# A two-layer diffusion trunk on one core: TensorE in program order, modulation in pairs of steps, a gate summed one stage earlier, and merged boundary evictions

## The chip, the core and the metric

The kernel runs on one core of a Trainium2 chip. The metric is the device time of one execution in microseconds (us), and the time of a kernel is the median of its runs. The core has five instruction streams that matter here: TensorE (PE, matrix products, with its weight loads shown apart as PEld), VectorE (DVE), ScalarE (ACT), GpSimd (POOL) and SyncE (SP, which only issues transfers). Each works through its own list of instructions in order and waits on semaphores for the others. On-chip data lies in SBUF; PE writes its results to PSUM, of which the kernel uses eight banks of 128 partitions x 512 fp32.

## The reference

The input is 512 "sample" tokens and 128 "prompt" tokens of width 1024. Two layers follow; each has a channel mixer, a token mixer (a gated recurrence, RG-LRU, in layer 0; windowed averages in layer 1) and a second channel mixer. Every mixer reads a normalised and modulated input and adds a gated, normalised output to the residual x:

```python
def _layer(x, mod, l, norm_g, ffn_w1, ffn_w3, ffn_w2, mixer):
    sh1, sc1, g1, sh2, sc2, g2, sh3, sc3, g3 = jnp.split(mod[:, None, :], N_MOD, axis=-1)
    h = _modulate(_rmsnorm(x, norm_g[l, 0]), sh1, sc1)                 # x * (1 + scale) + shift
    x = x + 0.5 * g1 * _rmsnorm(_swiglu(h, ffn_w1[l, 0], ffn_w3[l, 0], ffn_w2[l, 0]), norm_g[l, 1])
    h = _modulate(_rmsnorm(x, norm_g[l, 2]), sh2, sc2)
    y, st = mixer(h)                                                   # RG-LRU (l = 0), pool (l = 1)
    x = x + g2 * _rmsnorm(y, norm_g[l, 3])
    h = _modulate(_rmsnorm(x, norm_g[l, 4]), sh3, sc3)
    return x + 0.5 * g3 * _rmsnorm(_swiglu(h, ffn_w1[l, 1], ffn_w3[l, 1], ffn_w2[l, 1]), norm_g[l, 5]), st

def _swiglu(x, w1, w3, w2):      # D_MODEL 1024, D_FF 2816
    return (jax.nn.silu(x @ w1) * (x @ w3)) @ w2
```

`mod` is silu(c) @ mod_w[l] + mod_b[l]: nine vectors of 1024 per layer, for sample and prompt tokens. In the pool mixer each of four channel groups is replaced by (mean over a window - itself) @ pool_w, with windows 2, 4, 8 and 16 over an 8 x 64 grid of sample tokens and over the line of prompt tokens.

## The kernel before, in words

The 640 tokens are five tiles t of 128 (0 to 3 sample, 4 prompt). Six stages follow each other: channel mixer (0,0), RG-LRU (0,1), channel mixers (0,2) and (1,0), pool (1,1), channel mixer (1,2). Every fp32 operand of a large product is split into a rounded high part and the rest, and a product is three matmuls (low x high, high x low, high x high).

**Channel mixers.** The up-projections use Strassen-Winograd: each block of 128 hidden units has seven products of 128x320 (names A11, S2, S3, S1, A22, S4, A12; `mmP`, L498), made from two halves of the tokens (0 to 319, 320 to 639) and of the channels. Each product reads a weight that ACT (L136) and DVE (L137) have split beforehand. The down-projection (`mmB`, L580) is accumulated into y (tiles `yacc`) by DVE at L588, and the last four hidden blocks are left for the end (`final`).

**Boundaries.** `close` runs over the token tiles. For each: the last products, y += (DVE, L588), squares (ACT, L353), y*G by the gate (DVE, L379), 1/rms (DVE L347, then a power on POOL, L349), x += (DVE, L387), squares of x, a spill of x to memory (L395), its 1/rms, and the scaling (ACT, L399). Two tiles later `c_t` transposes the tile on PE (L476), evicts it with scale and shift (half on ACT, L484, half on DVE, L482) and splits it (L207 ACT, L208 DVE), and `h_sums` forms the Strassen sums. Then `ffn_start` runs the first products of the next mixer: A11 of four blocks, c_t(3), A12, c_t(4).

**Modulation.** A vector of `mod` is eight k-steps on PE, each of four 32x256 matmuls (L262; eight records in the trace) on one 512 KB tile `mw`, of which two exist; x tiles share them. `mod_step(2)` puts two steps between other products. A shift or scale vector then goes into columns (L276); a gate becomes a row, is split, and is broadcast by PE to the tile G (L304, evicted by ACT at L307). Bank `m` (one) serves all of this, beside four banks `q` and three `b`.

**Pool.** `pool_start` makes the group products (L950) and the split `qs`, `pool_rest` first finishes the gate (1,1), and then per token tile the window sums (L977), which are products with 0/1 matrices. Those come through tiles of kind `c` (two of them) and are copied by ACT at L936.

**Order.** The program text gives an order, but a scheduler places all instructions of all engines; a priority follows the program's order, and an instruction that is estimated to wait is passed by others.

Of the kernel before, what the change touches and what calls it, by code (L numbers as in the profile page):

```python
# [16 lines left out]
P = 128  # L17
# [66 lines left out]
class Kern:  # L84
# [40 lines left out]
    def weight_gen(self):  # L125
        nc = self.nc
        V = nc.vector
        for i, (kind, srcs, opt) in enumerate(self.entries):
# [14 lines left out]
            elif kind in ("full", "rest"):  # L143
# [10 lines left out]
                if kind == "full":  # L154
                    yield quarter(b21)
# [3 lines left out]
                yield quarter(t4)  # L159
                yield quarter(b22)  # L160
# [45 lines left out]
    def split(self, hi, lo, src):  # L206
        self.nc.scalar.activation(hi, src, AF.Copy)  # L207
        self.nc.vector.tensor_sub(lo, src, hi.bitcast(F32))  # L208
# [46 lines left out]
    def mod_gen(self):  # L255
        nc = self.nc
        for (l, s, kind) in self.mod_order:
            ps = self.p("m")
            for k in range(KC):
                w = self.mod_take()  # L260
# [3 lines left out]
                self.mod_dma()  # L264
                yield
            mrow = self.t("mrow", [P, 256])
            if kind < 2:
                nc.vector.tensor_copy(mrow, ps[:, 0:256])
                yield
                if kind == 0:  # L270
                    ab = self.t("ab", [P, 2, KC, 2])
                    self.ab[(l, s)] = ab
                ab = self.ab[(l, s)]
                pc = self.p("m")
                for q in range(2):
                    nc.tensor.matmul(pc[:, 8 * q:8 * q + 8], mrow[:, q * P:(q + 1) * P], self.col("sel"), start=True, stop=True)  # L276
                src = pc[:, 0:16].rearrange("p (q j v) -> p q j v", q=2, j=4)
                dst = ab[:, kind].rearrange("p (j q) v -> p q j v", q=2)
                mb = self.col("modb", (l * 6 + s * 2 + kind) * 16, 16).rearrange("p (j q v) -> p q j v", q=2, v=2)
                if kind == 0:  # L280
                    for q in range(2):
                        nc.vector.tensor_add(dst[:, q], src[:, q], mb[:, q])
                else:
                    gm = self.col("gam", (l * 3 + s) * 16, 16).rearrange("p (k v) -> p k v", v=2)
                    for q in range(2):
                        nc.vector.tensor_add(dst[:, q], src[:, q], mb[:, q])
                    nc.vector.scalar_tensor_tensor(ab[:, 1], ab[:, 1], 1.0, gm, op0=ALU.add, op1=ALU.mult)
            else:
# [7 lines left out]
                while self.g_busy:  # L296
                    yield "hold"
# [961 lines left out]
```

## Time and profile before

| | |
|---|---|
| median of 3 runs | 2238.29 us (2236.69 to 2248.3) |
| the profiled execution, its time and its span | 2239.14 us, 2236.9 us |
| busy: PE, DVE, ACT, POOL | 2117.5, 1701.5, 1012.9, 73.2 us |
| channel mixer (1,0) from its start to pool | about 1191 to 1690 us of the span |
| pool from its first boundary to the next mixer's seven products | about 1690 to 1806 us |

The span is counted from the first to the last instruction in the trace; what lies around it (2.2 us) is the launch. PE's busy time includes pipelined overlap with a modelled end, so a stage in which PE shows 377.00 of 377.00 us is one in which it never waits, not one at its peak. Idle time of an engine is followed by what ended it. In a timeline a row joins equal instructions that follow each other (x8), with the time from the first's start to the last's end.

### The profile page before, as it was taken

The numbers are of one execution on the slowest core, as the hardware profiler recorded it, in microseconds if no ns is written. First come the engines' busy times: TensorE is split into PE (matmuls) and PEld (weight loads), VectorE is DVE, ScalarE is ACT, GpSimd is POOL, SyncE is SP. The second block draws the span as 40 slices with busy tenths as digits, with TensorE's granted clock in tenths as the row PEclk, the third lists the DMA queues.
The fourth block names the chain that finished last, engine by engine and source line by source line (L and its number), as shares of the span: only waits on it lengthen the run. The fifth ranks groups of instructions, "written<-read, shape, count | busy, mean of one in ns | idle before, by whom it ended". The sixth has DMA issues, their size and how long they took to land.

```text
span 2236.9 us, 32742 instructions
## 1 busy us (share of the span) xinstructions
PE 2117.5 (95%) x13015; PEld 1897.3 (85%) x13015; DVE 1701.5 (76%) x2753; ACT 1012.9 (45%) x1779; POOL 73.2 (3%) x107
## 2 busy tenths in 40 slices
PE   6999999998999899999998899999998599999998
PEld 4888889987887789889997798888896488999997
DVE  5967777768988886777877967777777796787875
ACT  5443333348866744323335543332336754333332
POOL 0000000001211100000000000000001100000000
PEclk7999999999999899999999999999999799999999
DMA  8424332224235542442213623334335442222222
GB/s 278 170 99 142 132 104 95 76 100 159 96 114 163 186 156 81 145 142 85 87 67 122 211 86 123 132 132 142 135 115 174 167 170 99 77 93 76 78 73 94
DMA packets 72713, 278.26 MB, mean 124 GB/s; under 512 B 7392, under 2 KB 15600, under 8 KB 61296
## 3 DMA queue, kind: packets, MB, share of 16 engines
q1 hardware_dynamic: 72528, 276.16, 35.9%
q8 instruction: 102, 1.67, 0.3%
q14 instruction: 51, 0.42, 0.1%
q0 software_dynamic: 32, 0.01, 0.0%
HBM read 260.40 MB, written 15.74 MB: 123 GB/s over the span
## 4 chain that ended last, share of the span: by engine, by line
PE 77%; DVE 10%; ACT 5%; DMA 4%; issue 2%; POOL 1%; SPq 1%; POOLq 0%; DVEq 0%; ACTq 0%
PE q L498 43%; PE b L580 24%; PE m L262 3%; PE q L507 2%; PE b L498 2%; DMA mw<-in_mod_w_dram 2%; DVE mw L387 1%; DMA raw<-in_w_dram 1%; POOL st L349 1%; DVE wp L177 1%; DVE wp L137 1%; DVE h L208 1%; ACT yacc L399 1%; ACT mhl L353 1%; DVE h L824 1%
## 5 line engine op out<-in xcount | busy, mean ns | idle before, releaser
L498 PE MATMUL q<-h,wp 128*128 128x320 f32 x6912 | 1056.7, 313 | 13.1 <-DVE c L524 5.4
L498 PEld LDWEIGHTS q<-h,wp 128*128 128x128 f32 x6912 | 1029.6, 190 | 43.7 <-issue 16.9
L580 PE MATMUL b<-wp,g 128*128 128x512 f32 x2880 | 671.6, 392 | 3.7 <-DVE g L208 2.3
L580 PEld LDWEIGHTS b<-wp,g 128*128 128x128 f32 x2880 | 536.7, 188 | 124.1 <-issue 8.6
L136 ACT ACTIVATE wp<-raw 128x512 fp32r<-128x512 f32 x440 | 267.1, 628 | 617.2 <-PE b L580 300.0
L137 DVE TENSOR_TENSOR wp<-raw,wp 128x512 fp32r<-128x512 f32 x440 | 298.2, 688 | 115.5 <-ACT wp L136 114.0
L588 DVE TENSOR_TENSOR yacc<-yacc,b 128x512 f32<-128x512 f32 x380 | 258.6, 685 | 125.2 <-PE b L580 122.6
L177 DVE TENSOR_TENSOR wp<-raw,wp 128x1024 fp32r<-128x1024 f32 x118 | 144.3, 1223 | 67.0 <-PE q L498 58.9
L174 ACT ACTIVATE wp<-raw 128x1024 fp32r<-128x1024 f32 x94 | 99.6, 1060 | 158.0 <-PE q L498 147.9
L136 ACT ACTIVATE wp<-T 128x512 fp32r<-128x512 f32 x176 | 108.9, 626 | 104.1 <-PE q L498 103.9
L507 PE MATMUL q<-h,wp 128*128 128x320 f32 x768 | 122.3, 313 | 8.5 <-ACT h L207 6.1
L137 DVE TENSOR_TENSOR wp<-T,wp 128x512 fp32r<-128x512 f32 x176 | 118.5, 689 | 15.1 <-ACT wp L136 14.9
L507 PEld LDWEIGHTS q<-h,wp 128*128 128x128 f32 x768 | 115.5, 190 | 13.1 <-ACT h L207 6.3
L150 DVE TENSOR_TENSOR T<-raw 128x1024 f32<-128x1024 f32 x88 | 107.7, 1224 | 23.3 <-DMA raw<-in_w_dram 22.0
L262 PE MATMUL m<-mw,csil 128*32 128x256 f32 x1024 | 87.6, 393 | 13.9 <-DMA mw<-in_mod_w_dram 12.2
L349 POOL TENSOR_TENSOR st<-st,mhalf 128x1 f32<-128x1 f32 x60 | 40.0, 666 | 1558.2 <-DVE st L347 1549.7
L498 PEld LDWEIGHTS b<-h,wp 128*128 128x128 f32 x480 | 76.1, 201 | 15.6 <-ACT h L207 5.2
L498 PE MATMUL b<-h,wp 128*128 128x320 f32 x480 | 81.7, 327 | 7.1 <-ACT h L207 3.3
L207 ACT ACTIVATE g<-c 128x1280 fp32r<-128x1280 f32 x44 | 56.2, 1277 | 65.8 <-DVE c L564 65.8
L208 DVE TENSOR_TENSOR g<-c,g 128x1280 fp32r<-128x1280 f32 x44 | 65.5, 1488 | 8.9 <-ACT g L207 8.5
L558 ACT ACTIVATE c<-c 128x960 f32<-128x960 f32 x44 | 43.9, 998 | 57.0 <-DVE c L536 57.0
L262 PEld LDWEIGHTS m<-mw,csil 128*32 128x32 f32 x1024 | 27.8, 109 | 46.3 <-issue 20.5
(204 smaller groups left out, 1637.6 us busy)
## 6 DMA issues: line engine op xcount, KB each, us to landing
raw<-in_w_dram SPq DMA_DIRECT2D x88, 1024.0 KB, 4.8
mw<-in_mod_w_dram SPq DMA_DIRECT2D x130, 512.0 KB, 3.9
raw<-in_w_dram SPq DMA_DIRECT2D x88, 512.0 KB, 4.6
x_spill<-mw SPq DMA_DIRECT2D x25, 512.0 KB, 2.6
mw<-x_spill SPq DMA_DIRECT2D x25, 512.0 KB, 3.8
raw<-in_w_dram SPq DMA_DIRECT2D x32, 256.0 KB, 5.4
raw<-in_w_in_dram SPq DMA_DIRECT2D x16, 512.0 KB, 4.3
wp<-in_mod_w_dram SPq DMA_DIRECT2D x8, 512.0 KB, 9.6
```

What stands on the lines that cost most here:

```text
L136: nc.scalar.activation(w[:, 0:512], src, AF.Copy)
L137: V.tensor_sub(w[:, 512:D], src, w[:, 0:512].bitcast(F32))
L150: V.tensor_sub(T, raw[:, 512:1536], raw[:, 0:1024])
L174: nc.scalar.activation(wh, r, AF.Copy)
L177: V.tensor_sub(wl, r, wh.bitcast(F32))
L208: self.nc.vector.tensor_sub(lo, src, hi.bitcast(F32))
L262: nc.tensor.matmul(ps[32 * j:32 * j + 32, 0:256], self.csil[:, k, :], w[:, j * 256:(j + 1) * 256], start=(k == 0), stop=(k == KC - 1), til ...
L349: nc.gpsimd.tensor_tensor(rs, ms[:, 0:1], self.mhalf, op=ALU.pow)
L498: self.nc.tensor.matmul(out, a, b[:, k], start=(start and not onto and k == first and n == 0), stop=(stop and k == last and n == 2), skip_ ...
L507: self.nc.tensor.matmul(out, a[:, sl], b[k // 2][:, k % 2, cols], start=(n == 0), stop=(n == 3 * KC - 1))
L580: nc.tensor.matmul(pb, a[:, ts_], b[:, ns], start=(c == 0), stop=(c == 3 * len(fl) - 1))
L588: nc.vector.tensor_add(y, y, pb)
```

## The change

1. **Order of PE.** From the rest of mixer (0,0), and from the start of mixer (0,2) to the end, PE's instructions keep the program's order (`manual_schedule`); the RG-LRU stage and the other engines are scheduled as before.
2. **Modulation in pairs.** `mod_gen` gives way after two k-steps; `mod_step()` runs one such pair. The column work runs ahead of the next pair, and columns and broadcast use a bank `b`. One more `mod_step` stands in `ffn_start` and one per block in `rg_rest`. What is left of a stage's vectors is done behind tile 0 in `close`.
3. **Pool's gate.** The eight k-steps and the row of (1,1) are moved into mixer (1,0) (key `"row"`); pool itself keeps the split and the broadcast. In pool all ten window products come first, and the next tile is begun ahead of a tile's `res_close`.
4. **Boundaries.** Tiles 0 and 1 go through `c_t` as a pair (128x256 evictions), at a raised priority; tile 2 is evicted once at 128x128 and copied by POOL. `final` begins three of its accumulations with the first two hidden blocks. y*G for the first half of each tile, the low part of A22 and the sum f12 - s2 move from DVE to POOL. Within `seven_rest` one yield, and with it A12, moves behind A22; the weight b21 moves with it.

```diff
-        self.nc.vector.tensor_sub(lo, src, hi.bitcast(F32))                       # split
+        (engine or self.nc.vector).tensor_tensor(lo, src, hi.bitcast(F32), op=ALU.subtract)
...
             for k in range(KC):                                                   # mod_gen
+                if k % 2 == 0 and tail:
+                    tail()
+                    tail = None
+                    if self.m_use >= self.m_cap:
+                        yield
                 w = self.mod_take()
...
-                self.mod_dma()
-                yield
+                if k % 2:
+                    self.mod_dma()
+                    if k < KC - 1:
+                        yield
...
+                self.mod_done.add((l, s, "row"))
                 yield
                 while self.g_busy:
                     yield "hold"
+                mhl = self.t("mhl", [P, 2, 256], F32R)
+                self.split(mhl[:, 0], mhl[:, 1], mrow)
+                yield
+                self.g_busy = True
...
-        self.nc.vector.tensor_mul(y, y, self.G[(l, s)][:, v, n * 512:(n + 1) * 512])     # res_half
+        (self.nc.vector if n else self.nc.gpsimd).tensor_tensor(y, y, self.G[(l, s)][:, v, n * 512:(n + 1) * 512], op=ALU.mult)
...
-        self.h_put("A22", ks, cols, f22)                                          # h_sums
-        V.tensor_sub(f12, f12, s2)
+        self.h_put("A22", ks, cols, f22, self.nc.gpsimd)
+        self.nc.gpsimd.tensor_tensor(f12, f12, s2, op=ALU.subtract)
...
+        if first:                                                                 # close
+            for t in range(NT):
+                for n in range(2):
+                    product(t, n)
+            begin(0)
+        for t in range(NT):
+            if not first:
+                begin(t)
+            elif t + 1 < NT:
+                begin(t + 1)
             self.res_close(t)
+            if t == 0:
+                for m in self.phase_mods[l, s]:
+                    self.mod_until(*m)
             if nxt:
                 self.c_next(t)
-                if t >= 2:
-                    self.c_t(t - 2, *nxt)
+                if t == (1 if first else 3):
+                    with self.tc.high_priority(300):
+                        self.c_t((0, 1), *nxt)
+                elif t == (2 if first else 4):
+                    with self.tc.high_priority(300):
+                        self.c_t((2,), *nxt)
...
+        for t, n in ((0, 0), (0, 1), (1, 0)):                                     # final
+            begun[t, n] = self.mmB(t, n, fl[:2], ws[:2], False, total=total)
...
-        for m in self.phase_mods[l, s]:                                           # pool_rest
-            self.mod_until(*m)
+        self.mod_until(1, 1, 2)
-        self.close(self.pool_box, l, s, nxt)
+        self.close(self.pool_box, l, s, nxt, first=True)
...
-                           (0, 2): [...], (1, 0): [(1, 0, 2), (1, 1, 0), (1, 1, 1), (1, 2, 0), (1, 2, 1)],
+                           (0, 2): [...], (1, 0): [(1, 0, 2), (1, 1, 0), (1, 1, 1), (1, 2, 0), (1, 2, 1), (1, 1, "row")],
...
+        order = lambda: self.tc.manual_schedule(engines={mybir.EngineType.PE})    # run
...
+        with order():
+            self.ffn_start((0, 2, False), n)
```

How PE's instructions move at the boundary from mixer (0,2) to (1,0), before (L476 are transposes of a token tile, yacc its scaled tile; L498 products of the next mixer, `q` banks A11; L262 a modulation step):

```order
L476 MATMUL q_11304<-cols_64,yacc_7736 128x128 x4
L476 MATMUL q_11319<-cols_64,yacc_7736 128x128 x4
L476 MATMUL b_11384<-cols_64,yacc_7737 128x128 x4
L476 MATMUL b_11393<-cols_64,yacc_7737 128x128 x4
L498 MATMUL q_11335<-h_10988,wp_10945 128x320
L498 MATMUL q_11336<-h_10988,wp_10962 128x320
L498 MATMUL q_11337<-h_10988,wp_10978 128x320
L262 MATMUL m_11675<-mw_11676,csil_68 32x256
```

And with the change, where transposes are L489, products L524 and modulation L271 (rows of products between those shown left out):

```order
L489 MATMUL q_11272<-cols_64,yacc_7720 128x128 x4
L489 MATMUL q_11281<-cols_64,yacc_7720 128x128 x4
L524 MATMUL q_11297<-h_10985,wp_10923 128x320
...
L489 MATMUL b_11342<-cols_64,yacc_7721 128x128 x4
L489 MATMUL b_11351<-cols_64,yacc_7721 128x128 x4
L524 MATMUL q_11299<-h_10985,wp_10954 128x320
...
L489 MATMUL b_11435<-cols_64,yacc_7722 128x128 x4
L489 MATMUL b_11444<-cols_64,yacc_7722 128x128 x4
...
L271 MATMUL m_11518<-mw_11519,csil_68 32x256 x4
L271 MATMUL m_11518<-mw_11521,csil_68 32x256 x4
L524 MATMUL b_11537<-h_10989,wp_11393 128x320
```

Tile 3's transposes stood ahead of the first A11; they now stand behind two A11 products, and the modulation steps follow in one block behind A12 instead of among the products.

In pool, PE before, around the start of the window sums (L977) and the broadcast of the gate (L304):

```order
L977 MATMUL b_16102<-h_15746,g_15736 128x256
L977 MATMUL b_16102<-h_15748,g_15736 128x256
L262 MATMUL m_15959<-mw_15992,csil_68 32x256 x4
L977 MATMUL b_16102<-h_15750,g_15736 128x256
...
L977 MATMUL b_16155<-h_15749,g_15736 128x256
L304 MATMUL m_16017<-mhl_16013,bsel_71 128x256 x4
L977 MATMUL b_16155<-wp_15751,g_15736 128x256
```

With the change (L1009 the last group product, L301 the broadcast, L1036 the window sums):

```order
L1009 MATMUL b_15945<-wp_15724,h_15417 128x256
L1009 MATMUL b_15945<-wp_15384,h_15417 128x256
L301 MATMUL b_15964<-mhl_15960,bsel_71 128x256 x4
L301 MATMUL b_15970<-mhl_15960,bsel_71 128x256 x4
L301 MATMUL b_15976<-mhl_15960,bsel_71 128x256 x4
L301 MATMUL b_15982<-mhl_15960,bsel_71 128x256 x4
L1036 MATMUL b_16032<-h_15745,g_15728 128x256
L1036 MATMUL b_16032<-h_15744,g_15728 128x256
```

The modulation steps have left the stage, and the broadcast stands in one piece ahead of the first window sum.

POOL's list at the same mixer boundary as above, before (a power for each 1/rms, and nothing else):

```order
L349 TENSOR_TENSOR st_11146<-st_11110,mhalf_66 128x1
L349 TENSOR_TENSOR st_11155<-st_11150,mhalf_66 128x1
L349 TENSOR_TENSOR st_11219<-st_11183,mhalf_66 128x1
L349 TENSOR_TENSOR st_11228<-st_11223,mhalf_66 128x1
L349 TENSOR_TENSOR st_11290<-st_11254,mhalf_66 128x1
```

And with the change (L395 is y*G, L515 the copies of tile 2's part, L365 the power, L456 f12 - s2, L208 the low part of A22):

```order
L395 TENSOR_TENSOR yacc_7721<-yacc_7721,G_7940 128x512
L515 COPY c_10999<-yacc_11271 128x4x64
L515 COPY c_11000<-yacc_11271 128x4x64
L365 TENSOR_TENSOR st_11173<-st_11137,mhalf_66 128x1
L365 TENSOR_TENSOR st_11182<-st_11177,mhalf_66 128x1
L395 TENSOR_TENSOR yacc_7722<-yacc_7722,G_7940 128x512
L365 TENSOR_TENSOR st_11254<-st_11218,mhalf_66 128x1
L365 TENSOR_TENSOR st_11263<-st_11258,mhalf_66 128x1
L456 TENSOR_TENSOR c_11000<-c_11000,g_11270 128x4x64
L456 TENSOR_TENSOR c_11000<-c_11000,g_11270 128x4x128 x2
L208 TENSOR_TENSOR h_10998<-yacc_11271,h_10997 128x4x64
L208 TENSOR_TENSOR h_10998<-g_11268,h_10997 128x4x128 x2
```

The power of each tile's 1/rms now has a 128x512 product ahead of it, and the Strassen parts stand behind the last of them.

More of the change, by code (lines that the diff above doesn't have):

```diff
@@ L159, in weight_gen @@
                 yield quarter(t4)
+                if kind == "full":
+                    yield quarter(b21)
                 yield quarter(b22)
@@ L268, in mod_gen @@
                 nc.vector.tensor_copy(mrow, ps[:, 0:256])
+                tail = lambda a=(mrow, l, s, kind): self.mod_cols(*a)
                 yield
[L270 to L287, printed above, removed]
             else:
@@ new lines, in c_t @@
+        w = P * len(tiles)
+        n = 512 // w
+        sl = slice(t * P, t * P + w)
+        second = None
+        if not plain:
+            if t * P + w <= HT:
+                dst = lambda kk: self.F[0][kk // HK][:, kk % HK, sl]
+            else:
+                o = max(0, t * P - HT)
+                sums = slice(o, (t + 1) * P - HT)
+                if t * P < HT:
+                    self.f2 = [self.view(self.t("g", [P, 2 * TOK])) for _ in range(4)]
+                    hf = self.t("yacc", [P, D]).rearrange("p (k t) -> p k t", k=KC)
+                    dst = lambda kk: hf[:, kk]
+                    cut = HT - t * P
+                    second = [hf[:, 0:HK, cut:P], hf[:, HK:KC, cut:P]] + [x[:, :, sums] for x in self.f2[2:]]
+                else:
+                    dst = lambda kk: self.f2[kk // HK][:, kk % HK, sums]
+                    second = [x[:, :, sums] for x in self.f2]
+                self.sums[t] = self.h_sums(slice(0, HK), sums, second)
@@ L492, in mmP @@
+        if plain:
+            return
+        if second is None:
+            for j in range(2):
+                self.h_first(j, slice(0, HK), sl)
+        elif t * P < HT:
+            own = slice(t * P, HT)
+            for j, name in enumerate(("A11", "A12")):
+                self.h_put(name, slice(0, HK), own, hf[:, j * HK:(j + 1) * HK, 0:cut])
+            for j in range(2):
+                nc.gpsimd.tensor_copy(self.F[0][j][:, :, own], hf[:, j * HK:(j + 1) * HK, 0:cut])
     def mmP(self, out, h, w, ks=range(HK), start=True, stop=True, first=0, last=HK - 1, onto=False):
@@ L524, in seven_rest @@
         V.tensor_add(c12, p6, s1)
-        yield
         p7 = self.bank(tag)
@@ L600, in block_B, with close @@
         self.done(2 * len(fl), room)
-    def close(self, product, l, s, nxt):
+    def close(self, product, l, s, nxt, first=False):
         if nxt:
```

213 lines of the change are left out of this document (113 added, 100 removed).

## The prediction

> **What bounds the kernel now.** I read the busy shares and the chain that ended last first, then busy time by stage, then the waits of PE stage by stage, and the timeline only where PE waits.
>
> ```profile
> PE 2117.5 (95%) x13015; PEld 1897.3 (85%) x13015; DVE 1701.5 (76%) x2753; ACT 1012.9 (45%) x1779; POOL 73.2 (3%) x107
> PE 77%; DVE 10%; ACT 5%; DMA 4%; issue 2%; POOL 1%; SPq 1%; POOLq 0%; DVEq 0%; ACTq 0%
> ```
>
> Three quarters of the chain are PE's own work, so the kernel can lose time only by fewer or cheaper matmuls, or in the places where PE stands still. The view by windows shows where these are (per row: window and its length, then busy us of PE, PEld, DVE, ACT and POOL with their instruction counts, and PE's clock, DMA share, GB/s):
>
> ```profile
> 814.00:1191.00 377.00, 377.00 (x2302) 344.72 (x2303) 278.87 (x419) 136.94 (x212) 0.00 (x0) 1.00 0.30 104
> 1191.00:1286.00 95.00, 80.35 (x464) 67.09 (x462) 80.70 (x154) 57.99 (x131) 7.59 (x10) 0.93 0.49 168
> 1221.00:1252.00 31.00, 22.89 (x137) 19.84 (x137) 27.71 (x61) 24.25 (x60) 3.96 (x4) 0.83 0.49 156
> 1680.00:1840.00 160.00, 124.46 (x830) 107.31 (x829) 128.28 (x257) 109.16 (x256) 14.16 (x20) 0.90 0.51 174
> 1738.00:1754.00 16.00, 15.41 (x128) 13.04 (x128) 10.94 (x19) 9.64 (x20) 0.00 (x0) 1.00 0.68 237
> 1754.00:1788.00 34.00, 11.34 (x68) 9.65 (x67) 27.30 (x62) 29.13 (x76) 7.37 (x8) 0.62 0.40 142
> ```
>
> Inside a channel mixer (814 to 1191) PE never stands still. At the boundary of two mixers (1191 to 1286) it misses 14.65 us of 95, in pool and its boundary (1680 to 1840) 35.54 of 160. In the last row PE works 11.34 of 34 us, at a granted clock of 0.62, while ACT has 29.13 and DVE 27.30: there the epilogue of the token tiles is the bound. The waits of PE in pool (total, times, longest) and its wait for modulation tiles in the whole run:
>
> ```profile
> PE q L476 <- ACT yacc L399: 19.0, 4, 9.9
> PE b L476 <- ACT yacc L399: 4.9, 1, 4.9
> PE m L262 <- DMA mw<-in_mod_w_dram: 12.2, 11, 2.4
> ```
>
> **Pool, the largest term.** Rows of the timeline (start, length, idle time and its releaser):
>
> ```profile
> 1737.81 2.40 PE L950 MATMUL b<-wp,h 128*128 128x256 f32 x18
> 1740.13 0.64 PE L262 MATMUL m<-mw,csil 128*32 128x256 f32 x8
> 1740.70 1.21 PE L977 MATMUL b<-h,g 128*128 128x256 f32 x8
> 1743.44 0.83 ACT L985 ACTIVATE yacc<-b,cols 128x256 f32<-128x256 f32 x2
> 1745.34 0.64 PE L262 MATMUL m<-mw,csil 128*32 128x256 f32 x8 [0.21 <-DMA mw<-in_mod_w_dram]
> 1745.91 1.20 PE L977 MATMUL b<-h,g 128*128 128x256 f32 x8
> 1753.58 0.60 ACT L307 ACTIVATE G<-m 128x512 f32<-128x512 f32 x1 [0.82 <-PE m L304]
> 1754.07 0.62 ACT L353 ACTIVATE mhl<-yacc 128x512 bf16<-128x512 f32 x1
> 1768.41 3.20 POOL L349 TENSOR_TENSOR st<-st,mhalf 128x1 f32<-128x1 f32 x1 [3.19 <-DVE st L347]
> 1771.65 1.33 ACT L399 ACTIVATE yacc<-mw,st 128x512 f32<-128x512 f32 x2 [2.77 <-POOL st L349]
> 1772.42 1.97 PE L476 MATMUL q<-cols,yacc 128*128 128x128 f32 x8 [9.93 <-ACT yacc L399]
> 1779.03 1.97 PE L476 MATMUL q<-cols,yacc 128*128 128x128 f32 x8 [4.64 <-ACT yacc L399]
> 1785.91 1.97 PE L476 MATMUL b<-cols,yacc 128*128 128x128 f32 x8 [4.91 <-ACT yacc L399]
> 1787.73 11.80 PE L498 MATMUL q<-h,wp 128*128 128x320 f32 x72
> ```
>
> The last step of the gate runs at 1745.34; row, split, broadcast and its eviction follow, the last ending at 1754.18, and the first square of tile 0 starts at 1754.07, 13.4 us after the first window sum. The squares are scheduled behind the gate although they need only y. With the gate's steps gone, the broadcast runs ahead of the sums. The steps still between the group products (1740.13 to 1740.70, and some before) are gone too, so the first sum starts near 1739.5: not earlier, as the last group products end at 1740.2 and these wait for tile 4. Tile 0's two halves of y are there after its two window products and evictions: before, the first product ran from 1740.70, with a modulation step in it, until ACT's eviction at 1743.44 to 1744.27, 3.6 us in all; without the step, and with the second, smaller product behind it, the squares of both halves are due near 1739.5 + 4.4 = 1743.9. First part: 1754.07 - 1743.9 = 10.2 us.
>
> From the first square to A11 it is 1787.73 - 1754.07 = 33.7 us, with three tiles' epilogues and, ahead of A11, tile 3's transposes (1785.91, after 4.91 us of waiting). In the new order A11 of two blocks stands ahead of these; 4.91 + 1.82 = 6.7 us at most. Against it ACT, with 29.13 us in 34, also gets work that stood in the 16 us before, and the transposes of tile 0 now wait for tile 1 (the pair). I take 6 of the 6.7: **16 us** in all. Bounds: 6, if only A11's place counts because ACT still keeps tile 0's squares back; 24, if the stretched power at 1768.41 (3.20 us, where undisturbed ones take 0.55) and some 4.6 us of the wait for tile 2 go as well.
>
> **Modulation.** Steady rows in mixer (1,0), eight records a step:
>
> ```profile
> 1441.00 1.07 PE L262 MATMUL m<-mw,csil 128*32 128x256 f32 x16
> 1442.00 10.85 PE L498 MATMUL q<-h,wp 128*128 128x320 f32 x72
> ```
>
> Two steps in one block take 1.00 us from start to the next start; one alone takes 1745.91 - 1745.34 = 0.57. So a step costs 0.43, and a block 0.14 on top. The eight steps of the gate move into mixer (1,0), where PE never waits: 8 x 0.43 = +3.4. The runs of such matmuls in PE's order fall from 101 to 67; without pool's eight that is some 26 blocks x 0.14 = -3.6. The tiles arrive ahead of a pair, as two products (72 matmuls, 10.85 us) lie between pairs and a tile lands in 3.9:
>
> ```profile
> mw<-in_mod_w_dram SPq DMA_DIRECT2D x130, 512.0 KB, 3.9
> ```
>
> Of the 12.2 us of waits 3.4 lie in pool; the rest may shrink by pairs, or grow at the starts, where x tiles hold both buffers and PE can no longer pass a late pair. Sum -1 (from -6 to +4).
>
> **Boundaries.** The mixer boundary at 1221, and RG-LRU's:
>
> ```profile
> 1220.99 1.27 PE L476 MATMUL q<-cols,yacc 128*128 128x128 f32 x8 [0.27 <-ACT yacc L399]
> 1228.38 1.97 PE L476 MATMUL b<-cols,yacc 128*128 128x128 f32 x8 [6.12 <-ACT yacc L399]
> 1231.08 1.17 PE L498 MATMUL q<-h,wp 128*128 128x320 f32 x3 [0.73 <-ACT h L207]
> 1251.66 0.41 PE L498 MATMUL b<-h,wp 128*128 128x320 f32 x1 [0.81 <-ACT h L207]
> 754.30 1.97 PE L476 MATMUL b<-cols,yacc 128*128 128x128 f32 x8 [5.10 <-ACT yacc L399]
> L379 DVE TENSOR_TENSOR yacc<-yacc,G 128x512 f32<-128x512 f32 x60 | 41.3, 689 | 21.3 <-ACT mhl L353 21.1
> ```
>
> Two A11 products (24 matmuls; 72 take about 10.85 us, so 3.6) now fill the gap ahead of tile 3's transposes. Their operand needs tile 2's eviction and split behind 1220.99, near 1225. Tile 3 itself comes no earlier than DVE, busy 27.71 of 31 us here, lets it: but DVE hands five multiplies of 0.689 us to POOL, 3.4 us. Both readings give 3.5; whichever comes second is no further gain. Two boundaries: **-7** (0, where the in-order wait for tile 3 takes all back; -12, where the whole waits of 6.12 and 5.10 go and 1 us more). The transposes behind the two products are not passed now: later A11 products, their copies on ACT and the bank they hold wait with them.
>
> Mixer to RG-LRU: smaller evictions and the three begun accumulations, -1 (to -5). Between, ACT gets six more table loads (44 instead of 38 in its order):
>
> ```profile
> L786 ACT ACT_TABLE_LOAD x11 | 14.1, 1283 | 0.2
> ```
>
> 6 x 1.283 = 7.7 us on an engine that is busy 45% of the span; I take 0 and keep +7.7.
>
> Work on POOL has no row of its kind. It costs from 0.55 us (the undisturbed 128x1 power) upward. For its slope the nearest rows are two fills:
>
> ```profile
> L744 POOL MEMSET T<- 128x1 f32 x7 | 1.0, 148 | 488.7 <-DVE wp L137 433.2 <-DVE h L765 31.6 <-DVE c L765 23.9
> L1152 POOL MEMSET csil<- 128x256 f32 x1 | 0.3, 313 | 0.0
> L349 POOL TENSOR_TENSOR st<-st,mhalf 128x1 f32<-128x1 f32 x60 | 40.0, 666 | 1558.2 <-DVE st L347 1549.7
> ```
>
> (313 - 148) / 255 = 0.65 ns an element, so 0.55 + 512 x 0.65 ns = 0.88 us for a 128x512 product (an estimate; low end 0.55, high end the 3.20 of the stretched power plus 0.33 = 3.5). At 0.88 against DVE's 0.69, beside the second half's square (0.81 with its read), it delays a tile by about 0.1. I take that as nothing.
>
> The Trainium skill ("GPSIMD Engine Reference", section 3.1, elementwise accounting) gives 4497 ns for a 2048-wide fp32 product on GpSimd and 2293 on VectorE; a quarter, 1.1 us, is an estimate from that page, and by it each tile would come some 0.3 us later. That would leave the sum within 2 us.
>
> **Sum**, against the profiled execution: 2239.1 - 16 - 1 - 7 - 1 = **2214 us** (the median of the runs, 2238.3, is 0.8 lower). All low ends: 24 + 6 + 12 + 5 = 47, so 2192; all high ends: -6 + 4 + 0 + 7.7 = +6, so 2245.
>
> **Rivals.**
>
> *POOL is kept waiting by DVE (slower).* The power at 1768.41 took 3.20 us instead of 0.55; it ended only when a run of DVE instructions with two SBUF inputs did. DVE is busy 27 of 31 to 34 us at every boundary, mostly with such instructions, and the changed kernel gives POOL products that read two SBUF operands, ahead of the powers, and the A22 and S4 parts behind them. Price: PE waits for L399 at ten places of the whole run:
>
> ```profile
> PE q L476 <- ACT yacc L399: 19.2, 5, 9.9
> PE b L476 <- ACT yacc L399: 17.4, 5, 6.1
> ```
>
> Each would be later by the stretch x plus 0.88 - 0.69 = 0.19. And the six POOL parts (f12 - s2 and A22's low, for three tiles) at each of three mixer starts take 6 x (0.88 + x), of which S2, S3 and S1 (36 matmuls, 5.4 us) hide 5.3. At x = 1.3 (half of 2.65): 15 + 3 x 7.8 = 38, less 25 gained: 2252. It decides from x = 0.9. For it speaks that one power in ten of a boundary is stretched so; against it, that most are not (mean 0.67 us).
>
> This is what the Trainium skill states ("SBUF — State Buffer", section "Who interferes with whom"): a VectorE instruction with two SBUF inputs contends with a GpSimd one that reads SBUF. By that rule, the trace agrees with 3.20 us once; how long a 512-wide product would be held no run here shows.
>
> *The gate moves, the chain does not.* Transfers and copies of the 0/1 matrices, and ACT with 29.13 of 34 us, set the time to A11, so pool gains 6 and the boundaries 3: 2239 + 3.4 - 3.6 - 9 = 2230. For it: ACT's longest gap in those 34 us is 2.77.
>
> *Larger gain.* All low ends: DVE's and ACT's relief shortens every tile: about 2194.
>
> *No net change.* Program order on PE takes back at the mixers what the boundaries give: a late weight or pair stalls everything behind it, where the scheduler had filled the place; 2238. Against it: 377.00 of 377.00 us busy, so little was late there.
>
> **Chances.** Forecast 0.46 (2200 to 2227), larger gain 0.14, the gate without the chain 0.16, POOL 0.14, no net change 0.10. A measurement of this kernel tells about 0.5% (11 us) from no change: faster is below 2227, slower above 2249.5. Faster: 0.46 + 0.14 + half of 0.16 = 0.68; same: 0.08 + 0.10 + 0.03 of POOL's = 0.21; slower 0.11. The range runs from 2190 (below all low ends) to 2246; outside it lie POOL's 0.11 and some 0.04 of the larger gain.
>
> **What would show it.** Right: no modulation step between pool's group products and window sums; first square within 5 us of the first sum; from that square to A11 under 30 us; A11 ahead of tile 3's transposes at the boundaries, with S2 3 to 4 us sooner after the last product; POOL's 128x512 product near 0.9 us. Wrong: such products above 1.8 us, or PE waiting for POOL before A22 or S4; new waits of PE inside 814 to 1191, for L136, L137 or modulation tiles; ACT's table loads on the chain in RG-LRU.

## The result

The changed kernel took 2265.44 us (median of 4 runs, 2260.47 to 2267.01) against 2238.45 for the kernel before: a ratio of 1.0108, 95% interval 1.0074 to 1.0141. It is 27 us slower, where I forecast 24 faster, and lies outside the range.

Where the time went is read best between marks that both traces have: the starts of PE's products (there are as many of each kind in both kernels). All columns are of profiled executions, in us:

| stretch | before | changed | difference |
|---|---|---|---|
| opening, to the third block of mixer (0,0) | 126.9 | 131.8 | +4.9 |
| four mixers, third block to last down-projection | 1510.9 | 1493.8 | -17.1 |
| into RG-LRU, until 96 of its products have started | 29.6 | 34.3 | +4.7 |
| RG-LRU, from there to its last down-projection | 214.0 | 232.4 | +18.4 |
| mixers (0,2) and (1,0): from there to S2 | 61.4 | 61.8 | +0.4 |
| three mixers: S2 to the third block | 185.1 | 196.7 | +11.6 |
| pool: last down-projection to first window sum (group products) | 33.7 | 43.1 | +9.4 |
| pool: first window sum to A11 | 47.0 | 38.1 | -8.9 |
| mixer (1,2): A11 to S2 | 18.0 | 22.7 | +4.7 |
| end | 10.2 | 10.5 | +0.3 |

The page of the changed kernel, and its windows over a mixer's inside, a mixer boundary and pool (columns as in the prediction: busy us of PE, PEld, DVE, ACT, POOL, then clock and transfers):

```profile
PE 2107.5 (93%) x13015; PEld 1907.6 (84%) x13015; DVE 1683.7 (74%) x2655; ACT 1013.5 (45%) x1739; POOL 175.4 (8%) x165
PE 74%; DVE 14%; ACT 6%; issue 3%; POOL 2%; DMA 1%; SPq 0%; POOLq 0%; DVEq 0%; ACTq 0%
```

```profile
831.00:1213.00 382.00, 379.87 (x2375) 349.95 (x2373) 283.70 (x428) 140.76 (x215) 0.00 (x0) 1.00 0.32 111
1213.00:1308.00 95.00, 78.81 (x430) 67.84 (x429) 74.46 (x130) 54.81 (x119) 30.96 (x23) 0.89 0.40 142
1786.00:1812.00 26.00, 6.43 (x26) 5.17 (x26) 22.78 (x41) 20.51 (x50) 12.44 (x12) 0.66 0.54 182
```

The chain of waits has less PE and more DVE, ACT and POOL. At the boundary DVE has 6 us less to do than before (74.46 against 80.70), POOL 31 us instead of 7.6, and PE still works less. The waits of PE, which answer to those of the prediction:

```profile
PE q L489 <- ACT yacc L415: 23.3, 9, 6.3
PE q L524 <- ACT h L207: 16.0, 4, 7.8
PE b L608 <- DVE g L208: 10.5, 5, 8.0
PE b L524 <- DVE c L556: 10.4, 5, 4.1
PE b L1009 <- DVE h L208: 9.5, 4, 4.8
PE m L271 <- DMA mw<-in_mod_w_dram: 8.1, 7, 3.4
PE b L489 <- ACT yacc L415: 8.0, 5, 2.0
```

Of the waits that I had aimed at, two did shrink (`b` transposes from 17.4 to 8.0, modulation tiles from 12.2 to 8.1), and that of the `q` transposes grew from 19.2 to 23.3. New ones have come: for the split operands of the first products (L524 for h), for c in the first blocks, for g in RG-LRU, and for h in pool's group products (L1009).

### The profile page after: what moved, and what is told of

The parts are those of the page before. It is cut to its first block, busy times and chain, and to the rows that moved or that the text cites. A ratio compares the mean times of both kernels' runs of the same rounds, so it can differ in the third digit from the quotient of the medians.

```text
span 2265.2 us, 32719 instructions
## 1 busy us (share of the span) xinstructions
PE 2107.5 (93%) x13015; PEld 1907.6 (84%) x13015; DVE 1683.7 (74%) x2655; ACT 1013.5 (45%) x1739; POOL 175.4 (8%) x165
## 4 chain that ended last, share of the span: by engine, by line
PE 74%; DVE 14%; ACT 6%; issue 3%; POOL 2%; DMA 1%; SPq 0%; POOLq 0%; DVEq 0%; ACTq 0%
PE q L524 42%; PE b L608 24%; PE m L271 2%; PE b L524 2%; DVE wp L137 2%; PE q L533 2%; DVE h L208 1%; POOL st L365 1%; DVE mw L403 1%; DVE h L883 1%; DVE wp L177 1%; ACT yacc L415 1%; POOL c L456 1%; DVE T L150 1%; DVE yacc L395 1%
## 5 line engine op out<-in xcount | busy, mean ns | idle before, releaser
L524 PE MATMUL q<-h,wp 128*128 128x320 f32 x6912 | 1043.3, 312 | 24.9 <-ACT h L207 16.0
L524 PEld LDWEIGHTS q<-h,wp 128*128 128x128 f32 x6912 | 1026.2, 190 | 45.5 <-ACT h L207 17.2
L608 PE MATMUL b<-wp,g 128*128 128x512 f32 x2880 | 668.7, 392 | 11.6 <-DVE g L208 10.5
L395 POOL TENSOR_TENSOR yacc<-yacc,G 128x512 f32<-128x512 f32 x30 | 44.3, 1476 | 1320.5 <-ACT mhl L369 1320.4
L137 DVE TENSOR_TENSOR wp<-T,wp 128x512 fp32r<-128x512 f32 x176 | 118.0, 691 | 12.7 <-ACT wp L136 12.6
L524 PE MATMUL b<-h,wp 128*128 128x320 f32 x480 | 84.7, 336 | 26.7 <-DVE c L556 10.4
L524 PEld LDWEIGHTS b<-h,wp 128*128 128x128 f32 x480 | 78.8, 208 | 33.3 <-issue 14.1
L271 PE MATMUL m<-mw,csil 128*32 128x256 f32 x1024 | 71.4, 390 | 8.1 <-DMA mw<-in_mod_w_dram 8.1
L208 DVE TENSOR_TENSOR g<-c,g 128x1280 fp32r<-128x1280 f32 x44 | 65.4, 1485 | 9.5 <-ACT g L207 9.4
L584 ACT ACTIVATE c<-c 128x960 f32<-128x960 f32 x44 | 44.0, 1000 | 43.1 <-DVE c L562 43.1
L152 DVE TENSOR_TENSOR raw<-raw,T 128x512 f32<-128x512 f32 x88 | 61.2, 695 | 0.1
```

The lines of the kernel that those rows point to most:

```text
L137: V.tensor_sub(w[:, 512:D], src, w[:, 0:512].bitcast(F32))
L208: (engine or self.nc.vector).tensor_tensor(lo, src, hi.bitcast(F32), op=ALU.subtract)
L271: nc.tensor.matmul(ps[32 * j:32 * j + 32, 0:256], self.csil[:, k, :], w[:, j * 256:(j + 1) * 256], start=(k == 0), stop=(k == KC - 1), til ...
L395: (self.nc.vector if n else self.nc.gpsimd).tensor_tensor(y, y, self.G[(l, s)][:, v, n * 512:(n + 1) * 512], op=ALU.mult)
L524: self.nc.tensor.matmul(out, a, b[:, k], start=(start and not onto and k == first and n == 0), stop=(stop and k == last and n == 2), skip_ ...
L608: nc.tensor.matmul(pb, a[:, ts_], b[:, ns], start=(c == 0), stop=(c == total - 1))
```

## The experiments

Experiments 1 to 3 take one part away from the changed kernel (the second run of 3 starts from the kernel before). Their medians stand beside 2265.4, their ratios to the kernel before, with 95% intervals, beside 1.0108. Lengths of stretches are between the marks of the table above.

**1. POOL's work back on DVE.** Edit (lines shortened), and the second kernel with only the last two lines of it:

```diff
-        (self.nc.vector if n else self.nc.gpsimd).tensor_tensor(y, y, G, op=ALU.mult)
+        self.nc.vector.tensor_tensor(y, y, G, op=ALU.mult)
-        self.h_put("A22", ks, cols, f22, self.nc.gpsimd); self.nc.gpsimd.tensor_tensor(f12, f12, s2, op=ALU.subtract)
+        self.h_put("A22", ks, cols, f22); V.tensor_sub(f12, f12, s2)
```

> The changed kernel with y*G, A22's low part and f12 - s2 back on DVE; POOL keeps the powers and the six small copies. Theory 1 (POOL is held up by DVE, and A22, S4 and the powers are late for it): the subtraction of 9.16 us at mixer (1,0) is gone, and from S2 to block 2 the three mixer starts return from 55.3, 53.8 and 60.0 us to about 50, 50 and 56, mixer (0,0) saves about 4: 2265 - 16 = 2249. Theory 2 (PE in program order cannot pass what is late): at most 3 us better, 2262, since DVE gets the work back. Theory 3 (RG-LRU's modulation stands too early): RG-LRU's +20 us stays in this run, whichever of the others holds.

> The changed kernel with only A22's low part and f12 - s2 back on DVE; y*G of each first half stays on POOL. Theory 1: this is where the wait of PE for c (3.5 us at mixer (1,0)) came from, so two thirds of the first run's gain, about 2265 - 11 = 2254, and S2 itself stays 3 to 5 us late. If instead y*G on POOL is the late part: 2262, and the first run alone gains. Theory 2: 2263.

Measured: 2255.6 (1.0076, 1.0049 to 1.0102) and 2255.9 (1.0079, 1.0056 to 1.0101). So the part is 7 to 10 us, less than I expected, and all of it is A22's and S4's; y*G on POOL makes no difference. (The intervals of the ratios overlap that of the changed kernel; the single executions, 2253 to 2259 against 2260 to 2267 us, do not, and experiment 6 finds the same size again.) What holds them up is in the trace of the changed kernel. POOL at the start of mixer (1,0) (start, length):

```profile
1264.26 2.40 POOL L365 TENSOR_TENSOR st<-st,mhalf 128x1 f32<-128x1 f32 x1 [3.20 <-DVE st L363]
1266.63 1.96 POOL L456 TENSOR_TENSOR c<-c,g 128x256 f32<-128x256 f32 x2
1273.14 9.16 POOL L456 TENSOR_TENSOR c<-c,g 128x512 f32<-128x512 f32 x1 [4.55 <-DVE g L449]
1282.95 2.98 POOL L208 TENSOR_TENSOR h<-g,h 128x512 fp32r<-128x512 f32 x2
```

and DVE and ACT in the same stretch (rows between left out):

```profile
1276.60 0.68 DVE L452 TENSOR_TENSOR c<-c,g 128x512 f32<-128x512 f32 x1
1278.74 1.28 DVE L208 TENSOR_TENSOR h<-c,h 128x512 fp32r<-128x512 f32 x2
1279.95 1.21 DVE L150 TENSOR_TENSOR T<-raw 128x1024 f32<-128x1024 f32 x1
1282.33 0.63 ACT L207 ACTIVATE h<-c 128x512 fp32r<-128x512 f32 x1 [3.54 <-POOL c L456]
1282.99 1.79 DVE L208 TENSOR_TENSOR h<-c,h 128x512 fp32r<-128x512 f32 x1 [1.83 <-ACT h L207]
```

The subtraction at 1273.14 takes 9.16 us; it ends 1.1 us after DVE's unbroken run of instructions with two SBUF inputs, which lasts to 1281.2. Where POOL is first (1282.95), DVE's subtraction takes 1.79 us instead of 0.68. ACT has waited 3.54 us for POOL's result and DVE 1.83 us for ACT's; the sums c stand behind that in DVE's list, and PE waits 3.53 us for one of them (L556) in that first block. This fits the lock that the Trainium skill describes ("SBUF — State Buffer", section "Who interferes with whom": an exclusive lock, and issue order, not the shape of the operation, decides who blocks); the trace agrees in both directions, with 9.16 us on POOL and 1.79 us on DVE.

**2. Modulation in RG-LRU spread again.** Each block has two turns for a pair, and the change adds a third in six of the eight blocks. The first edit takes out the added turn and, in every second block, one of the other two; the second takes out only the added turn, and places what is left ahead of the last down-projection:

```diff
                 self.done(2, 4)
-                self.mod_step()
...
-            self.mod_step()                      # first edit only
+            if c % 2:
+                self.mod_step()
...
             self.rg_y(KC - 1)
+        for m in self.phase_mods[0, 1]:          # second edit only
+            self.mod_until(*m)
```

> The changed kernel with modulation in RG-LRU spread as before: the added pair per block is taken out and the second pair runs in every other block only, so the steps last to the end of the stage. Theory 3 (steps pulled forward displace products that the gates wait for, and no longer fill the wait ahead of the last down-projection): the wait of 7.97 us for g is filled, the waits for modulation tiles (4.4 us) shrink, RG-LRU is 8 to 13 us shorter: 2265 - 10 = 2255. If the table loads or the merged evictions make the stage longer: 2264, and the wait for g stays.

> The changed kernel with two pairs per RG-LRU block instead of three (16 turns for the 14 that the stage's three vectors need) and what is left placed ahead of the last down-projection, not inside close. Theory 3 mended: the earlier run was slow because steps were left over for close, where x tiles hold both of their buffers. Then RG-LRU between its 96th product and its last down-projection takes 232.4 - 8 = 224 us, 2257 in all, and table loads return to 36. If the place of modulation is not what makes the stage longer: 232 and 2265.

Measured: 2269.9 (1.0134, 1.0098 to 1.0170), no better; and 2249.4 (1.0045, 1.0030 to 1.0059), 16 better. In the first, too few turns were left, and the rest fell into `close` (RG-LRU 242.2 us). In the second RG-LRU takes 216.6 us, and ACT's table loads there are 36 again instead of 42. Of the 15.8 us that the stage gains, 11.6 are in two waits of PE: for modulation tiles 1.4 us instead of 8.1, for g 3.1 instead of 8.0. What the six loads have in the rest was not separated. What the added pair does, on PE of the changed kernel:

```profile
577.61 0.64 PE L271 MATMUL m<-mw,csil 128*32 128x256 f32 x8 [3.42 <-DMA mw<-in_mod_w_dram]
658.34 1.07 PE L271 MATMUL m<-mw,csil 128*32 128x256 f32 x16
730.24 4.28 PE L608 MATMUL b<-wp,g 128*128 128x512 f32 x18
742.49 11.85 PE L608 MATMUL b<-wp,g 128*128 128x512 f32 x42 [7.97 <-DVE g L208]
```

and at the same place of the kernel before:

```profile
710.73 4.15 PE L580 MATMUL b<-wp,g 128*128 128x512 f32 x17
716.88 0.64 PE L262 MATMUL m<-mw,csil 128*32 128x256 f32 x8 [2.00 <-DMA mw<-in_mod_w_dram]
717.45 1.27 PE L580 MATMUL b<-wp,g 128*128 128x512 f32 x3
718.65 1.08 PE L262 MATMUL m<-mw,csil 128*32 128x256 f32 x8
```

Before, the last steps stood in the wait for the last gate; with the change the last of them ran at 658 us, several of the earlier ones after a wait for their tile (3.42 us at 577.61), and PE stood still for 7.97 us where they had been. ACT does six more loads in the loop that the gates follow.

**3. PE placed by the scheduler**, in the changed kernel, and PE in program order alone on the kernel before:

```diff
-        order = lambda: self.tc.manual_schedule(engines={mybir.EngineType.PE})
+        order = nullcontext
```

> The changed kernel with PE placed by the scheduler again, everything else as changed. Theory 2 (program order exposes late operands): the starts of the mixers lose their extra waits, 3 x 5 us, and the steady parts stay: 2250. Theory 1 (POOL): the late operands stay late, PE fills some 2 us at each start: 2259, or worse where the scheduler puts modulation between products again (0.14 us a block, up to +4): 2265.

> The kernel before with one thing added: PE in program order in the channel mixers and pool. If program order is itself what costs (24 us in the run that took it away from the changed kernel): the boundaries and first blocks lose as much, 2238 + 20 = 2258 or more, since modulation stands at single steps there. If program order hurts only together with the merged evictions and POOL's parts: 2238 to 2242.

Measured: 2241.4 (1.0019, 1.0000 to 1.0039), 24 better; and 2320.6 (1.0355, 1.0324 to 1.0385), 82 worse. Without program order the opening is 127.8, the way into RG-LRU 28.6, S2 to the third block 186.6 and pool's group products 32.1 us: each of these four is within 2 us of the kernel before or better. RG-LRU (232.4) and A11 to S2 of mixer (1,2) (22.6) stay as long as in the changed kernel, and the four mixers from third block to last down-projection become 8 us longer (1501.8), all of it behind their last up-projection. So program order is the largest single loss. On the text of before it is far worse, and at another place: 49 of the 82 us lie inside the mixers, which are 9.6 to 16.0 us longer each (mixer (0,0) 389.0 instead of 377.3), and most of the rest in pool.

**4. Three undone together**: scheduler, A22's parts on DVE, two pairs per block with the rest ahead of the last down-projection.

> The changed kernel with three things undone: PE placed by the scheduler again, A22's low part and f12 - s2 on DVE, and no added pair per block in RG-LRU, with the rest of that stage's modulation ahead of its last down-projection. If the three costs are separate they add to the 2241.4 of the run without program order: -10 (POOL, as in the runs that took it off) and -8 (the wait for g): 2223, faster than both kernels. If the scheduler already passes what POOL delays: 2233. If RG-LRU's 18 us are not the modulation's place: 2231.

Measured: 2225.7 (0.9941, 0.9917 to 0.9965), faster than both. From here the other parts were taken out of this kernel one by one.

**5. Evictions tile by tile; y*G and tile 2's copies on DVE; program order only inside the mixers, from the third block to the last but the final down-projection.** The edit of the first:

```diff
-                if t == (1 if first else 3): ... self.c_t((0, 1), *nxt)
-                elif t == (2 if first else 4): ... self.c_t((2,), *nxt)
+                if t >= 2:
+                    self.c_t((t - 2,), *nxt)
```

> The combined kernel (scheduler on PE, A22's parts on DVE, two pairs per RG-LRU block; 2225.7) with the merged boundary evictions undone: tiles 0, 1 and 2 go through c_t one by one, two tiles behind, at ordinary priority. If merging saves what it removes (the evictions of a pair, tile 2's halves): 2225.7 + 6 = 2232. If the pair costs as much by waiting for tile 1 (A11 to S2 after pool took 2.9 us more in the combined kernel than before): 2222 to 2226.

> The combined kernel with POOL's remaining new work, y*G of each first half and tile 2's copies, back on DVE. y*G takes 1.29 us on POOL against 0.69 on DVE, but beside the second half's square. If that is off the path: 2226 within noise (the two runs without A22's parts, with and without it, were 2255.9 and 2255.6). If DVE is the bound at the boundaries and needs the relief: 2226 + 5 = 2231. If the longer product delays each tile: 2222.

> The combined kernel with PE in program order only inside the channel mixers, from the third block on to the last but the final down-projection. If program order costs at the boundaries alone, where operands come late, this is the same as the combined kernel or up to 2 us better: 2224 to 2226. If it also costs inside the mixers: 2230 or more.

Measured: 2220.1 (0.9916, 0.9898 to 0.9934), 2227.6 (0.9949, 0.9933 to 0.9965), 2230.6 (0.9958, 0.9942 to 0.9974). By the medians merging the evictions costs 5.6 us, but the intervals of the ratios overlap, so the loss is likely and not certain. Nor is its place shown: with the pair A11 to S2 of mixer (1,2) takes 20.9 us, tile by tile 17.1, while from the last down-projection to A11 in pool the pair takes 69.7 and tile by tile 80.0. y*G on POOL is worth nothing that can be told. Program order inside the mixers brings nothing on this text; their insides are as long (373.9 and 374.4 us in mixer (0,2)). The 5 us more are not clear of noise; most of them lie between S2 and the third block (191.5 against 185.3).

**6. On the kernel of 2220.1: A22's parts to POOL again, program order again, window products tile by tile (without the early start of the next tile).**

> The best kernel so far (scheduler on PE, single evictions, A22's parts on DVE; 2220.1) with A22's low part and f12 - s2 on POOL again. On the changed kernel these parts cost 10 us, with PE in program order. If POOL's lateness costs by itself: 2220 + 10 = 2230. If it costs only where PE cannot pass it, the scheduler's order hides most: 2220 to 2223.

> The best kernel so far with PE in program order again, and nothing else. Taken from the changed kernel, program order was worth 24 us, from the kernel before, with its text, 82 us the other way. If it is program order that costs, whatever else is there: 2220 + 20 = 2240. If it cost only through POOL's late parts and the merged evictions: 2220 to 2225.

> The best kernel so far with pool's window products taken tile by tile, as before, instead of all ten first; the gate stays a stage ahead. If all products first is what shortens pool (squares of tile 0 sooner, next tile begun early): from the first group product to A11 5 us more, 2225. If the gate alone did it: 2218 to 2221.

Measured: 2229.0 (0.9964, 0.9944 to 0.9984), 2238.7 (1.0003, 0.9989 to 1.0017), 2220.5 (0.9914, 0.9889 to 0.9940). POOL's lateness costs 9 us by itself, also when the scheduler may pass it; program order costs 18.6 by itself; all window products first is worth nothing in the whole time. What PE waits for with program order, whole run:

```profile
PE q L524 <- ACT h L207: 30.4, 4, 9.2
PE b L1006 <- DVE h L208: 15.4, 6, 5.6
PE q L489 <- ACT yacc L415: 14.2, 7, 5.3
PE b L524 <- DVE c L556: 11.2, 6, 3.6
PE b L489 <- ACT yacc L415: 7.7, 1, 7.7
PE q L524 <- DVE c L556: 5.7, 8, 1.0
```

and without it:

```profile
PE b L489 <- ACT yacc L415: 21.9, 5, 7.7
PE q L489 <- ACT yacc L415: 14.8, 8, 4.9
PE b L1006 <- DVE h L208: 11.8, 5, 5.3
PE q L524 <- ACT h L207: 9.3, 3, 6.2
PE q L524 <- DVE c L550: 4.0, 4, 1.2
PE b L524 <- DVE c L550: 2.4, 1, 2.4
```

In program order PE waits 21 us longer for the operand of the first products and some 11 us longer for c in the blocks (17 against 6), and 15 us less ahead of the transposes (21.9 against 36.7): the wait has moved from the transposes to what stands behind them, and grown.

**7. What shortened the mixers.** Their insides had lost 17.1 us, and no run had touched that. One kernel goes back to single steps, two of them at each place; one puts A12 and its weight back behind S2 (the lines of A12):

```diff
         V.tensor_add(c12, p6, s1)
+        yield                       # A12 runs at this place
         p7 = self.bank(tag)
...
         V.tensor_sub(c21, c21, p4)
-        yield
```

> The best kernel (2220.1) with modulation given way after every k-step again, two turns at a place, instead of one turn of two steps. The mixers' steady parts became 17 us shorter in the changed kernel with 4 steps more in them, where I had worked out 3.6 us for fewer blocks. If pairs bring that (40 blocks fewer, 0.4 us each): the steady parts go back by 10 to 17 us, 2230 to 2237. If two turns at one place stay together anyway: 2220 to 2223.

> The best kernel with A12 (and its weight) back at its old place behind S2, instead of behind A22. If the place of A12 is what made the steady parts shorter (PE waited 5.4 us for c behind S2 before): up to 8 us back, 2228. If the pairs did it: 2220 to 2222.

Measured: 2226.4 (0.9927, 0.9909 to 0.9945) and 2236.3 (0.9979, 0.9969 to 0.9989). The place of A12, with its weight, is worth 14 to 16 us. The pairs do not shorten the insides: mixer (0,0) takes 372.6 us with single steps and 372.7 with pairs, and the other three are 1.8 to 2.0 us shorter with single steps. The 6 us more lie elsewhere, 5 of them in RG-LRU and 7 between S2 and the third block, and the two ratios' intervals overlap. A block of seven times two products on PE (168 matmuls), of the kernel before:

```profile
1980.39 25.21 PE L498 MATMUL q<-h,wp 128*128 128x320 f32 x168
```

of the changed kernel:

```profile
1972.68 24.81 PE L524 MATMUL q<-h,wp 128*128 128x320 f32 x168
```

and of the one with A12 at its old place:

```profile
1939.23 25.22 PE L524 MATMUL q<-h,wp 128*128 128x320 f32 x168
```

0.40 us a block; with nine such blocks in each of four mixers, 14.4. It does not show among the waits of PE, and PE is busy all the time by the windows. From the starts of the matmuls, at two places of a block the step to the next one takes 0.25 us instead of 0.15, and some others up to 0.05 more. The weight loads, which wait ahead of the matmuls, show it in their groups over 1950 to 2190 us (busy, mean | idle before); with the old place:

```profile
L524 PEld LDWEIGHTS q<-h,wp 128*128 128x128 f32 x1061 | 157.0, 188 | 2.3 <-ACT c L570 0.9
```

and with the new one, in the kernel of 2220.1:

```profile
L524 PEld LDWEIGHTS q<-h,wp 128*128 128x128 f32 x1008 | 148.4, 188 | 0.5
```

L570 is ACT's copy of A11's result out of the bank onto which A12 accumulates. In the steady blocks of mixer (1,2) of the kernel with the old place, a weight load stands idle for 0.16 us until that copy ends (at 2071.65 in one of them, and the load starts at 2071.70), and another, at S4, for 0.10 us until DVE's sum from the bank of S1 ends (L557, at 2066.05; the load starts at 2066.11), as S4 accumulates onto that bank. The second wait is too short for the views to name. With the new place both are gone: A12 stands between A22 and S4 and leaves ACT and DVE the time. That is 0.26 of the 0.40 us; the other 0.14, some small steps more, remain open.

**8. Parts of the change alone on the kernel before**: the gate, A12's place, and both.

> The kernel before with only the gate of pool summed a stage ahead. By my working the squares of tile 0 come 10 us earlier and the steps cost mixer (1,0) 3.4 + 8 x 0.14 = 4.5: 2238 - 6 = 2232. If ACT and the copies set the time to A11 anyway: 2238 to 2242. The changed kernel without program order showed 37.5 us from the first window sum to A11 instead of 47.0; by that, -5.

> The kernel before with only A12 and its weight moved behind A22. In the steady blocks of before and of the kernel with the old place, two of seven products of a unit start 0.1 us late (24.90 us a block against 24.50): 9 blocks x 4 mixers x 0.40 = 14.4, so 2224. If the place frees a wait only in combination: 2235.

> The kernel before with two pieces of the change and nothing else: the gate of pool a stage ahead (alone 2232, ratio 0.996) and A12 with its weight behind A22 (taken out of the best kernel it cost 14 to 16 us). If both are gains by themselves: 2238 - 8 - 15 = 2215, below the best kernel so far (2220). If A12's place gains only with pairs of steps: 2230.

Measured: 2232.2 (0.9959, 0.9944 to 0.9974), 2226.0 (0.9956, 0.9939 to 0.9972), and 2208.9 together (0.9880, 0.9861 to 0.9898). The last is the fastest kernel of all, 29 us under the one before and 56 under the changed one, and it is the kernel before with some ten lines moved. The gate alone saves 13.5 us in pool and gives half of it back: with its eight steps mixer (1,0) takes 398.0 us instead of 391.1, 4.3 of the difference behind the last up-projection. With both, pool takes 31.9 us to the first window sum and 36.2 from there to A11, 12.6 less than before, and mixer (1,0), with the steps added, is still 2.7 us shorter.

## Why the prediction was wrong

The step that failed is the one that gave program order on PE no cost of its own. The sum let it take back the 7 us of the boundaries and a few us at the modulation tiles at most, and the rival that charged it the whole gain, "No net change", was set aside because PE is busy 377.00 of 377.00 us inside a mixer, "so little was late there". It cost 19 to 24 us, at the operands of the first products and at c. Two terms of the sum were mis-sized as well: RG-LRU's steps, put at 0, cost 14 to 16, and pool, put at -16, came to +0.5. Together with POOL's parts and perhaps the merged evictions that is more than the gain from the place of A12, which the sum did not hold at all.

**Pool, forecast -16: the first part came and was lost again one stretch earlier; the second did not come.** The changed kernel has the first square 4.5 us behind the first window sum (13.4 before), as worked out, and gains 8.9 us from that sum to A11. The other 6 of the 16 are not there: from the first square to A11 it is 33.6 us, as before (33.7). And the group products, which I let end where they did, take 9.4 us more. The gate's broadcast (1770.96 to 1773.36) now stands in that stretch, the granted clock is 0.76 there instead of 0.95, and PE in program order waits for each tile's operand: it stands 14.4 us instead of 8.9, up to 4.75 at once. With the scheduler the stretch is 32.1 again. On the kernel before, the gate alone takes 67.3 us from the last down-projection to A11 instead of 80.8, so the move is worth 13.5 there, and its steps cost mixer (1,0) 7.0 where I had worked out 3.4. The stretch by windows, before and changed, and rows of PE in the changed kernel:

```profile
1707.00:1740.70 33.70, 24.76 (x194) 19.45 (x192) 24.83 (x56) 28.42 (x70) 2.30 (x4) 0.95 0.72 230
1730.30:1773.36 43.06, 28.63 (x162) 26.66 (x161) 26.71 (x56) 30.09 (x71) 7.02 (x6) 0.76 0.38 124
```

```profile
1739.17 4.79 PE L1009 MATMUL b<-wp,h 128*128 128x256 f32 x24 [3.87 <-DVE yacc L618]
1751.37 2.93 PE L1009 MATMUL b<-wp,h 128*128 128x256 f32 x12 [4.75 <-DVE h L208]
1797.86 3.46 PE L489 MATMUL q<-cols,yacc 128*128 128x128 f32 x15 [6.29 <-ACT yacc L415]
1811.47 5.50 PE L524 MATMUL q<-h,wp 128*128 128x320 f32 x24 [2.64 <-ACT h L207]
```

**Boundaries, forecast -3.5 each: right at A11, nothing at S2.** From the last down-projection A11 came 3.1 and 4.2 us sooner, but S2 0.2 sooner and 0.5 later. I took the gap ahead of tile 3's transposes for free time; the operands of S2 come no earlier, and in program order PE waits for them itself. What moved the wait to the next place is named in my text ("wait with them") and has no price there. The merged evictions, which I put under "smaller evictions, -1", brought nothing and by the medians cost 5.6.

**RG-LRU, forecast 0, kept +7.7.** I priced six table loads, and they came (44 instead of 38 in the whole trace, 42 instead of 36 in this stage). I did not price the added pair: steps that had filled the wait for the last gate were pulled ahead, to where they waited for their tiles. Cost of it all, the loads included: 14 to 16 us. Of a step that is moved I counted its time, but not what it had covered.

**Modulation, forecast -1.** With eight steps more inside, mixer (1,0) is 3.1 us shorter where (0,0) and (0,2) are 4.6 shorter, so the steps cost some 1.5 us, and the pairs showed no gain inside the mixers: as small as worked out in the sum, but the 3.6 that pairs were to save is not seen (experiment 7). But beside them stood the place of A12, which my working left out: -14 to -16, and -10 to -12 alone on the kernel before. A stage in which PE is busy 377.00 of 377.00 us, and of which I wrote that PE never waits, still held some 1% of pauses, a tenth or two of a microsecond each, too short for the view; I read it as full.

**POOL, the rival: right in kind, too dear.** The stretch came (9.16 us once, 3.66 on average over six subtractions); the price for its six parts at three starts was 23 and measured 7 to 10. I take it that S2, S3 and S1 hid more; that was not tested. y*G and the powers behind it, priced at 15, cost nothing that can be told: y*G takes 1.26 to 1.30 us undisturbed, where I worked out 0.88, and up to 3.57 beside DVE, but it stays off the path. (The estimate from the Trainium skill, "GPSIMD Engine Reference", section 3.1, was 1.1, nearer, and still low.)

```profile
L395 POOL TENSOR_TENSOR yacc<-yacc,G 128x512 f32<-128x512 f32 x30 | 44.3, 1476 | 1320.5 <-ACT mhl L369 1320.4 <-POOL st L365 0.2
L456 POOL TENSOR_TENSOR c<-c,g 128x512 f32<-128x512 f32 x6 | 21.9, 3657 | 11.0 <-DVE g L449 11.0
```

**"No net change" by program order** was the rival nearest to the truth, and I gave it a tenth. Against it I held the full inside of a mixer. That was no argument: 377.00 of 377.00 us were measured with PE placed by the scheduler, which had filled the places, and the same text in program order is 9.6 to 16.0 us longer inside each mixer (experiment 3). On the changed text, with A12 moved and steps in pairs, program order costs nothing inside (experiment 5) and 19 to 24 us where the stages meet.

The accounts close to within some 10 us: program order 19 to 24, the added pair 14 to 16, POOL's parts 7 to 10, merging 5.6 (not certain) are 46 to 56; the kernel without them is 45 faster than the changed one. The differences of single stretches are less sure than that: pool's group products, which the edit of A22's parts does not touch, took 37.9 us in that run against 43.1, I take it because the scheduler places the other engines anew for each kernel; and the opening took 125.1 us in the kernel of 2220.1 and 128.7 with the window products tile by tile, an edit far behind it. Verdicts here rest on whole times; stretches only say where.

## What to carry to other kernels

Judge an order on an engine by the places where its operands come late. A stage that is full under one order says nothing about another: the scheduler may have filled it. Before moving work earlier, look for the wait that it has been filling. A change of many parts should be taken apart even when it is slower: here two small parts were worth 29 us and all the rest cost 56.

## What the runs showed of the hardware

A POOL instruction of 128x512 with two SBUF inputs took 1.26 us alone and up to 9.16 us beside an unbroken run of DVE instructions with two SBUF inputs; a DVE subtraction that came second took 1.79 us instead of 0.68. Pauses of 0.1 to 0.2 us in PE's stream added up to 14 us of 2240 and showed in no wait of PE, only in the idle time of its weight loads and in the length of a block of 168 matmuls (25.21 against 24.81 us). Two of them per block, 0.26 of 0.40 us, were weight loads of products that accumulate onto a bank from which ACT or DVE was still reading; the cause of the rest stays open.
